# A two-layer hybrid decoder: the last projection turned to token order, single copies of cumulative sums, two float32 weight tiles for four, and another order in the mixers

## The chip, the cores and the metric

The kernel runs on one core of a Trainium2 chip. The metric is device time in microseconds (us) of one execution; lower is better. TensorE does the matrix products (PE in the profile, PEld for the load of its stationary operand), VectorE (DVE) and ScalarE (ACT) the elementwise work, GpSimd (POOL) a few fills, and SyncE (SP) issues all DMAs.

## The reference

A decoder trunk of two layers on 272 tokens (16 learned ones in front of 256), width 1024, float32. Each layer is a half-step SwiGLU, a mixer of three kinds of heads that run side by side, and another half-step SwiGLU, each followed by a LayerNorm of alpha times the stream plus the new part:

```python
for l in range(DEPTH):                                   # DEPTH = 2
    h = layer_norm(ALPHA * h + 0.5 * swiglu(h, gate1, up1, down1), ln1_g, ln1_b)
    proj = h @ w_in[l]
    z, xbc, dt_raw, fq, fk, fv, f_raw, cq, ckv, k_rope = split(proj)
    y_ssd = ssd_mixer(z, xbc, dt_raw, ...)               # state space, 8 heads, causal convolution before
    y_fox = fox_mixer(fq, fk, fv, f_raw, ...)            # attention with a forgetting bias, 4 heads
    y_mla = mla_mixer(cq, ckv, k_rope, ...)              # attention over latent keys, 4 heads
    mix = concatenate([y_ssd, y_fox, y_mla]) @ w_out[l]
    h = layer_norm(ALPHA * h + mix, ln2_g, ln2_b)
    h = layer_norm(ALPHA * h + 0.5 * swiglu(h, gate2, up2, down2), ln3_g, ln3_b)
return h[:, 16:]                                         # the 16 learned tokens are dropped
```

## The kernel before

Activations lie feature by feature: 128 features on the partitions, 272 tokens along the row, 8 such tiles for the width (22 for the inner width of a SwiGLU). A product takes 128 x 128 weights as the stationary operand and 272 tokens as the moving one; in layer 1 some run on 256 tokens, since the learned ones are no longer needed. To get near float32 from the faster float32r format, weights and activations are split into a high and a low part, and `pe3` (lines 363 to 365) makes three products for one: high by high, low by high, high by low. The split of weights is two instructions per 512 columns: a cast on ACT (`whi<-wraw`) and a subtraction on DVE (`wlo<-wraw,whi`). Four tiles of the mixers' input projection (`WHOLE`) are not split: `pe` (line 353) multiplies them as plain float32, and each such product stands in the trace as two records.

All instructions are put in order when the program is built, by a small scheduler (`Issue`). The program's parts are generators that hand it operations; it keeps a queue for each engine, takes the ready one of lowest priority number (`PR`), and gives an operation that may run on several engines to the one that it holds for least loaded. What comes out is a fixed order for each engine. On the chip an engine works its list in that order and waits where an operand isn't ready. The names in this document: `MORDER` is the order in which the tiles of the input projection are computed, `NUI` the number of those that start before the LayerNorm's statistics are known (they are corrected afterwards from two extra columns, hence 274 columns), `NUF` the same for pairs of gate and up tiles of a SwiGLU; `YORDER` is the order in which the eight parts of the mixers' output enter the output projection (0 to 3 state space, 4 and 5 the forgetting attention, 6 and 7 the latent attention), and `NPRE` the number of output tiles whose first four parts are multiplied ahead, as filler between the attention's steps.

In a mixer, `steps` turns one tile into softplus values (`sp`) by a chain of some 25 small operations; a product with a mask gives their running sums (`cu`). `copied` copies one row of these sums to all partitions by a product with a picked column (`cuh,identr` and `cul,identr`, lines 373 and 374). `Ct,Bt` are the scores of the state space, `m,z` its output products, `km,qm` and `fk,fq` the attention scores, `cs,s` transposes of probabilities, `sM,...` and `sT,...` the products with values, `inv,scr` the sums of squares of a root mean square, and `diag,ones` spreads one number per token over all partitions.

The last SwiGLU's down projection is made as all others: 8 output tiles by 22 inner tiles by 3 products of 256 columns. The LayerNorm after it (`Norm` with `last`) sums the tiles and their squares along the way (`zs`, `q`), multiplies both by a column of 1/1024, takes a square root on ACT and one Newton step, spreads the result, and scales the eight tiles on DVE, ACT and POOL; six DMAs write them.

Of the kernel before, what the change touches and what calls it, by code (L numbers as in the profile page):

```python
# [8 lines left out]
F32 = mybir.dt.float32  # L9
F32R = mybir.dt.float32r  # L10
# [6 lines left out]
P = 128  # L17
# [22 lines left out]
PR = dict(tail=2, shift=0, finish=0, means=1.5, whole=4, gated=3, front=0, soon=1, later=8, copies=5, head=4,  # L40
          meta=4, pair=7, state=1, group=7, steps=5, rope=1, linear=7, latent=8, conv=5.5, gate=0, query=4.5,
          scores=7.5, bytoken=0)

NSOON = 2
# [3 lines left out]
NUF, NUI = 6, 7  # L48
# [3 lines left out]
NPRE = 2  # L52
YORDER = (0, 1, 6, 7, 4, 5, 2, 3)
# [12 lines left out]
for _name, _w in (  # L66
# [50 lines left out]
class Issue:  # L117
# [5 lines left out]
    LAG = 0.13  # L123
# [42 lines left out]
    def resume(self, p):  # L166
# [6 lines left out]
        if isinstance(r, list):  # L173
            p[2] = len(r)
            for op in r:

                lag = 0.0 if op.eng == "t" and p[3] == "t" else self.LAG
# [111 lines left out]
def hybrid_trunk(ctx: ExitStack, tc: tile.TileContext, xt, wgu1, wd1, wgu2, wd2, win, wuq,  # L289
# [69 lines left out]
    def pe3(ps, a, b, start, stop):  # L359
# [7 lines left out]
        return Op("t", 3 * (ps.shape[-1] / 2400 + 0.0125), fn)  # L367

    def pe2(ps, a, bh, bl):


        def fn():
# [3 lines left out]
        return Op("t", 2 * (ps.shape[-1] / 2400 + 0.012), fn)  # L376
# [7 lines left out]
    for l in range(DEPTH):  # L384
        def plan_ffn(n, wgu, wd):
# [7 lines left out]
        plan_ffn(1, wgu1, wd1)  # L393
# [9 lines left out]
        plan_ffn(2, wgu2, wd2)  # L403
# [23 lines left out]
    def chunk(i, key, src, n, whole):  # L427
# [7 lines left out]
        yield D.dma_start(raw[:, :n], in_=src)  # L435
# [59 lines left out]
    identr = cpool.tile([P, 12], F32R, name="identr")  # L495
# [24 lines left out]
    def constants():  # L520
        yield [D.dma_start(pv, in_=pvec), D.dma_start(cs, in_=cst)]
        yield S.copy(identr, ident[:, :12])
# [36 lines left out]
    def spread(col, t0, sign, eng=("vgs",) * 3):  # L559

# [4 lines left out]
        for i, (a, b) in enumerate(token_tiles(t0)):  # L565
# [4 lines left out]
            ops.append(either(*[op for op in turn if op.eng in eng[i]]))  # L570
# [8 lines left out]
    class Norm:  # L579
# [4 lines left out]
        def __init__(self, l, which, coef, t0, u, x, last=False):  # L584
            self.l, self.which, self.coef, self.t0, self.u, self.x, self.last = l, which, coef / ALPHA, t0, u, x, last
# [21 lines left out]
        def front(self, t, ps):  # L607

            zt = z[:, t, self.tk]
            if self.last and t == 0:  # L610
                yield S.activation(self.st, ones[:, :8], AF.Sqrt)
# [4 lines left out]
        def tail(self, i):  # L616
# [4 lines left out]
            if self.last and i == KD - 1:  # L621
                self.mark("rest", 0)
                spawn(self.finish(zi, sq), PR["finish"])
            ops = [square(sq, zi)]
            if not self.last:
                g = pcol(self.l, self.which + "_g", i)
                uh, ul = self.u[0][:, i, self.tk], self.u[1][:, i, self.tk]
                ops.insert(0, scaled(uh, zi, g))
            yield ops
            if not self.last:  # L630
                yield V.scalar_tensor_tensor(ul, zi, g, uh.bitcast(F32), ALU.mult, ALU.subtract)
            self.mark("u", i)
            if self.last and i == KD - 1:
                self.mark("rest", 1)
                return
# [13 lines left out]
        def finish(self, *rest):  # L649
# [5 lines left out]
            spawn(self.means(*rest), PR["means"])  # L655

            nb = 2 * k if rest else 1
            yield take("bank", nb)
            pm = [bank() for _ in range(k)] if rest else [bank()] * k
            pq = [bank() for _ in range(k)] if rest else pm  # L660

            def sums(to, s, i, start, stop):
                a, b = tt[i]
                return to[i][:b - a, i:i + 1], s[:, a - self.t0:b - self.t0], inv[:, 0:1], start, stop

            tiles = range(k)
            po = [p[:, 4:] for p in pq]
            if rest:
                yield self.need(*[("sum", j) for j in range(KD - 1)], ("rest", 0))
                yield pe(*[sums(pm, self.zs, i, True, False) for i in tiles],  # L670
                         *[sums(po, self.q, i, True, False) for i in tiles],
                         *[sums(pm, rest[0], i, False, True) for i in tiles])
                yield self.need(("rest", 1))
                yield pe(*[sums(po, rest[1], i, False, True) for i in tiles])
                self.mark("msums")
                give("scr")
            else:
                yield pe(*[sums(pm, self.zs, i, True, True) for i in tiles],
                         *[sums(po, self.q, i, True, True) for i in tiles])
            msq, var = self.st[:, 0, :k], self.st[:, 1]  # L680
            if rest:
                parts = [(slice(0, P), slice(i, i + 1)) for i in tiles]
            yield [S.activation(msq[p, c], pm[c.start][p, c], AF.Square) for p, c in parts]
            yield [V.tensor_sub(var[p, c], po[c.start][p, c], msq[p, c]) for p, c in parts]
            give("bank", nb)
            var = var[:, :k]
            yield V.tensor_scalar(var, var, 0.0, EPS / ALPHA ** 2, op0=ALU.max, op1=ALU.add)
            r = yield from rsqrt(var, k, self.last)
            self.mark("root")
            if self.last:  # L690
                self.r = yield from spread(r, self.t0, 1.0, "vv")
                self.mark("stats")
                return
# [11 lines left out]
        def means(self, *rest):  # L705
# [3 lines left out]
            if not rest:  # L709
                yield pe((ps, ones, self.zs, True, True))  # L710
                yield scaled(self.nm, ps, -1.0 / 1024)
                give("bank")
                self.mark("nm")
                return
            yield self.need(*[("sum", j) for j in range(KD - 1)], ("rest", 0))
            yield pe((ps, ones, self.zs, True, False))
            yield self.need(("msums",))
            yield pe((ps, ones, rest[0], False, True))
            self.sums = ps
            yield S.mul(self.nm, ps, -1.0 / 1024)  # L720
            for ts in ((4, 6), (6, 8)):
                spawn(self.centred(*ts), PR["whole"] + 0.1 * ts[0])
            yield self.need(("root",))
            spawn(self.centred(0, 4), PR["whole"])

        def several(self, a, ts):

# [895 lines left out]
```

## Time and profile before

| what | value |
|---|---|
| runs | 1100.49, 1103.49 and 1104.07 us; median 1103.49 |
| profiled execution | 1102.75 us; its span from first to last instruction 1101.0 us |
| TensorE busy | 1081.2 us of the span (98%) |
| VectorE, ScalarE, GpSimd busy | 745.2, 620.4 and 7.3 us |
| granted TensorE clock, mean | 0.99 |
| DMA | 157 GB/s over the span, all on one queue of SP |

Busy time of TensorE counts a matmul from its start to its modelled end. Matmuls overlap, so a stretch can be busy throughout and still hold fewer matmuls than another of the same length; the number of matmuls in a stretch says more than the busy share. The granted clock is 1.0 at 2.4 GHz and 0.5 at 1.2 GHz.

### The profile page before, as it was taken

The page shows a single profiled execution, that of the slowest core. Times are in us where ns is not written, and L with a number is a line of the kernel's source. Part 1 is how long each engine was busy: PE and PEld are TensorE (multiplying, and loading weights), DVE is VectorE, ACT ScalarE, POOL GpSimd, SP SyncE. Part 2 cuts the span into 40 slices and gives each one's busy share as a digit, 9 for nine tenths or more (in the row PEclk, how much of TensorE's full clock was granted, in tenths as well). Part 3 has the DMA queues.
Part 4 walks back from the last instruction along what each step waited for, and adds up shares of the span by engine and source line. Part 5 has one row for each costly group of instructions (what it writes and reads, how often), then busy time and mean ns, then how long its engine had stood idle before and what let it go on. Part 6 is the DMA issues. An engine that isn't in the chain of part 4 may idle for free.

```text
span 1101.0 us, 21395 instructions
## 1 busy us (share of the span) xinstructions
PE 1081.2 (98%) x8340; PEld 1053.9 (96%) x8340; DVE 745.2 (68%) x1749; ACT 620.4 (56%) x1448; POOL 7.3 (1%) x18
## 2 busy tenths in 40 slices
PE   8999999999999999999999999999999999999996
PEld 8999999988979999999999999999899799999995
DVE  5655556688778985555679555565888589755563
ACT  6544444466876664444566444444768667645541
POOL 0000000000000000000000000000000000000000
PEclk9999999998999999999999999999999999999998
DMA  8655556515314275556526655564262153755641
GB/s 286 230 173 173 167 173 177 173 57 177 109 52 135 90 229 195 176 159 175 184 97 214 205 173 165 171 183 154 66 200 90 39 173 123 248 185 180 178 142 39
DMA packets 50997, 173.86 MB, mean 158 GB/s; under 512 B 5584, under 2 KB 8272, under 8 KB 50896
## 3 DMA queue, kind: packets, MB, share of 16 engines
q1 hardware_dynamic: 50896, 172.50, 49.8%
q8 instruction: 65, 1.06, 0.4%
q14 instruction: 36, 0.29, 0.1%
HBM read 171.43 MB, written 1.05 MB: 157 GB/s over the span
## 4 chain that ended last, share of the span: by engine, by line
PE 93%; ACT 4%; DVE 2%; issue 0%; DMA 0%; SPq 0%; DVEq 0%; ACTq 0%
PE bank L363 28%; PE bank L365 28%; PE bank L364 28%; PE bank L353 7%; ACT s L279 1%; PE bank L355 1%; DVE wlo L279 1%; DMA wraw<-in_wgu_dram 0%; ACT whi L279 0%; ACT km L279 0%; ACT scr L279 0%; DVE z L279 0%; ACT sT L279 0%; DVE scr L279 0%; PE bank L373 0%
## 5 line engine op out<-in xcount | busy, mean ns | idle before, releaser
L279 ACT CAST whi<-wraw 128x512 fp32r<-128x512 f32 (+2 forms) x648 | 376.0, 607 | 354.1 <-issue 278.4
L279 DVE TENSOR_TENSOR wlo<-wraw,whi 128x512 fp32r<-128x512 f32 (+2 forms) x648 | 421.7, 673 | 184.8 <-ACT whi L279 183.0
L363 PE MATMUL bank<-x0h,whi 128*128 128x272 f32 (+3 forms) x1220 | 353.2, 290 | 2.9 <-ACT whi L279 1.6
L365 PE MATMUL bank<-x0l,whi 128*128 128x272 f32 (+3 forms) x1220 | 350.5, 287 | 0.2
L364 PE MATMUL bank<-x0h,wlo 128*128 128x272 f32 (+3 forms) x1220 | 349.4, 286 | 0.5 <-DVE wlo L279 0.3
L363 PEld LDWEIGHTS bank<-x0h,whi 128*128 128x128 f32 x1220 | 231.1, 189 | 5.0 <-ACT x0h L279 2.5
L365 PEld LDWEIGHTS bank<-x0l,whi 128*128 128x128 f32 x1220 | 230.5, 189 | 1.3 <-DVE x0l L279 1.3
L364 PEld LDWEIGHTS bank<-x0h,wlo 128*128 128x128 f32 x1220 | 230.4, 189 | 1.3 <-DVE wlo L279 1.1
L363 PE MATMUL bank<-hh,whi 128*128 128x272 f32 (+1 forms) x704 | 202.3, 287 | 0.0
L365 PE MATMUL bank<-hl,whi 128*128 128x272 f32 (+1 forms) x704 | 201.3, 286 | 0.0
L364 PE MATMUL bank<-hh,wlo 128*128 128x272 f32 (+1 forms) x704 | 201.1, 286 | 0.0
L363 PE MATMUL bank<-x1h,whi 128*128 128x272 f32 (+3 forms) x592 | 174.0, 294 | 0.0
L365 PE MATMUL bank<-x1l,whi 128*128 128x272 f32 (+3 forms) x592 | 171.6, 290 | 0.0
L364 PE MATMUL bank<-x1h,wlo 128*128 128x272 f32 (+3 forms) x592 | 171.5, 290 | 0.0
L364 PEld LDWEIGHTS bank<-hh,wlo 128*128 128x128 f32 x704 | 132.6, 188 | 0.0
L363 PEld LDWEIGHTS bank<-hh,whi 128*128 128x128 f32 x704 | 132.5, 188 | 0.0
L365 PEld LDWEIGHTS bank<-hl,whi 128*128 128x128 f32 x704 | 132.5, 188 | 0.0
L363 PEld LDWEIGHTS bank<-x1h,whi 128*128 128x128 f32 x592 | 113.2, 191 | 0.5
L364 PEld LDWEIGHTS bank<-x1h,wlo 128*128 128x128 f32 x592 | 113.2, 191 | 0.3
L365 PEld LDWEIGHTS bank<-x1l,whi 128*128 128x128 f32 x592 | 113.3, 191 | 0.0
L279 DVE TENSOR_TENSOR scr<-scr,bank 128x272 f32<-128x272 f32 (+1 forms) x70 | 30.4, 434 | 68.7 <-PE bank L365 68.7
L279 DVE SCALAR_TENSOR_TENSOR z<-bank,hs 128x272 f32<-128x272 f32 (+1 forms) x48 | 20.9, 435 | 36.6 <-PE bank L365 36.4
(241 smaller groups left out, 945.9 us busy)
## 6 DMA issues: line engine op xcount, KB each, us to landing
wraw<-in_wgu_dram SPq DMA_DIRECT2D x174, 512.0 KB, 4.1
wraw<-in_wd_dram SPq DMA_DIRECT2D x64, 448.0 KB, 3.4
wraw<-in_win_dram SPq DMA_DIRECT2D x40, 512.0 KB, 3.4
wraw<-in_wd_dram SPq DMA_DIRECT2D x32, 512.0 KB, 3.5
wraw<-in_wout_dram SPq DMA_DIRECT2D x16, 512.0 KB, 3.7
wraw<-in_wuq_dram SPq DMA_DIRECT2D x2, 512.0 KB, 3.5
cs<-in_cst_dram SPq DMA_DIRECT2D x1, 856.5 KB, 6.9
hs<-in_xt_dram SPq DMA_DIRECT2D x3, 272.0 KB, 5.5
```

The lines of the kernel that those rows point to most:

```text
L279: op = Op(self.eng, self.cost(name, out, aps), lambda: getattr(self.to, name)(out, *args, **kw), table)
L353: nc.tensor.matmul(j[0], j[1], j[2], start=j[3], stop=j[4])
L355: nc.tensor.transpose(*j)
L363: nc.tensor.matmul(ps, a[0], b[0], start=start, stop=False)
L364: nc.tensor.matmul(ps, a[1], b[0], start=False, stop=False)
L365: nc.tensor.matmul(ps, a[0], b[1], start=False, stop=stop)
```

## The change

The down projection of the last SwiGLU is made by token (`by_token`): the stationary operand is a block of 128 tokens by 128 inner features, and the moving one 512 columns of weights, so that two blocks of tokens by two halves of the width fill four banks. The weights come in chunks of 4 output tiles by 2 inner ones, in rows of 256 floats. The stream is transposed into token order (`turned`), the LayerNorm is taken along the row with `bn_stats`, and each quarter of a block is transposed back, scaled and written by four DMAs. The last `NLAST` = 4 chunks are computed first for one block, then for the other. `copied` makes one product for two: the high part lies on rows 0 to 11 and the low part on rows 32 to 43 of one tile (`cub`), and the picked column (`both`) has a one in each. Two float32 tiles remain of four. `MORDER`, `YORDER`, the priorities, `NUF`, `NUI` and `NPRE` differ, and the scheduler holds a wait of 0.2 us instead of 0.13 behind an operation of TensorE.

```diff
-NSOON = 2
+NSOON = 3
-NUF, NUI = 6, 7
+NUF, NUI = 7, 8
+NLAST = 4
+LOW = 32
-NPRE = 2
-YORDER = (0, 1, 6, 7, 4, 5, 2, 3)
+NPRE = 3
+YORDER = (0, 7, 1, 6, 4, 3, 2, 5)
-MORDER = (M_Z + 3, M_Z + 1, M_B, M_FK, M_XS + 2, M_CQ, M_XS + 1, M_SMALL, M_XS + 3, M_CQ + 1, M_C, M_CKV, M_Z, M_XS,
-          M_FQ + 1, M_Z + 2, M_FV, M_FQ, M_FV + 1, "uq", "ukv", M_FK + 1)
-WHOLE = (M_SMALL, M_XS + 3, M_CQ + 1, M_C)
+MORDER = (M_XS + 1, M_Z + 1, M_CKV, M_Z + 3, M_CQ, M_XS + 2, M_XS, M_Z + 2, M_B, M_SMALL, M_FK, M_XS + 3, M_Z, M_CQ + 1, M_C, M_FK + 1, M_FQ + 1, M_FV, M_FV + 1, "uq", "ukv", M_FQ)
+WHOLE = (M_SMALL, M_C, )
...
-    LAG = 0.13
+    LAG, DRAIN = 0.13, 0.2
...
-            nc.tensor.matmul(ps, a, bh, start=True, stop=False)
-            nc.tensor.matmul(ps, a, bl, start=False, stop=True)
+    def pe1(ps, a, b):
+        return Op("t", ps.shape[-1] / 2400 + 0.0125, lambda: nc.tensor.matmul(ps, a, b, start=True, stop=True))
...
+            if last:
+                for h in range(2):
+                    for c in range(KF // 2):
+                        plan((l, n, "d", h, c), wd[l, 4 * h:4 * h + 4, :, 2 * c * P:2 * (c + 1) * P]
+                             .rearrange("d p c -> p d c"), 8 * P)
+                return
...
-            yield scaled(cuh[R], cu)
-            yield V.tensor_sub(cul[R], cu, cuh[R].bitcast(F32))
+            yield scaled(cub[R], cu)
+            yield V.tensor_sub(cub[LOW:LOW + 12], cu, cub[R].bitcast(F32))
```

`by_token` is new. `turned` transposes four tiles into a bank and copies them to `zt`; `front` adds a bank to it and takes the statistics; `quarter` normalises, transposes back and scales:

```python
def front(b, h, ps):
    zs = zt[:, b, h * 512:(h + 1) * 512]
    yield need((key, "turned", b, h))
    yield V.scalar_tensor_tensor(zs, ps, coef, zs, ALU.mult, ALU.add)
    give("bank")
    yield Op("v", 0.6, lambda: nc.vector.bn_stats(st[:, b, h], zs))
    mark(key, "stats", b, h)
...
def products(c, bs):
    w = [t.rearrange("p (d k x) -> p k d x", d=4, k=2) for t in weights[l, n, "d", h, c]]
    for i in range(2):
        k = 2 * c + i
        yield need(((l, "ffn", n), k), *[("w", (l, n, "d", h, c), j) for j in range(8)])
        for b in bs:
            a = [t[:, k, b * P:(b + 1) * P] for t in (hh, hl)]
            yield pe3(banks[b].rearrange("p (d x) -> p d x", d=4), a, [t[:, i] for t in w], k == 0, k == KF - 1)
```

How the instructions move, at three places. Line numbers differ by one between the two programs.

TensorE in the mixers of layer 0, before, from the running sums' products (`cs,sp`) on, with the last row in front of them:

```order
L365 MATMUL bank<-x1l,whi 128x272
L353 MATMUL bank<-cs,sp 12x272
L353 MATMUL bank<-cs,sp 12x144
L353 MATMUL bank<-cs,sp 12x16
...
L355 MATMUL bank<-cs,cu 128x12 x4
L355 MATMUL bank<-cs,cu 16x12 x2
L353 MATMUL bank<-Ct,Bt 128x272
L353 MATMUL bank<-Ct,Bt 128x144
L353 MATMUL bank<-Ct,Bt 16x16
L353 MATMUL bank<-inv,scr 128x1 x2
L353 MATMUL bank<-inv,scr 16x1
```

The left-out rows are six products of a projection tile. The same place in the change; the left-out rows are products of projection tiles (6, 9 and 9) and transposes `cs,xs`:

```order
L366 MATMUL bank<-x1l,whi 128x272
L354 MATMUL bank<-cs,sp 12x272
L354 MATMUL bank<-cs,sp 12x144
L354 MATMUL bank<-cs,sp 12x16
L356 MATMUL bank<-cs,xs 128x128 x4
...
L356 MATMUL bank<-cs,cu 128x12 x4
L356 MATMUL bank<-cs,cu 16x12 x2
...
L354 MATMUL bank<-Ct,Bt 128x272
L354 MATMUL bank<-Ct,Bt 128x144
L354 MATMUL bank<-Ct,Bt 16x16
```

The small products that stood together are now apart, with tiles of the projection between them, and the sums of squares (`inv,scr`) no longer stand here.

TensorE at the end of the mixers of layer 1, before, where the last head's probabilities (`cs,s`) are transposed and multiplied with the values; `x0h` with `whi` is the output projection:

```order
L355 MATMUL bank<-cs,s 128x128 x5
L353 MATMUL bank<-sM,df 128x256
L353 MATMUL bank<-sT,vf 128x256
L353 MATMUL bank<-sT,vf 128x128
L353 MATMUL bank<-sT,vf 128x256
L353 MATMUL bank<-sT,vf 128x128
L363 MATMUL bank<-x0h,whi 128x256
```

The same place in the change:

```order
L356 MATMUL bank<-cs,s 128x128 x2
L364 MATMUL bank<-x0h,whi 128x256
L365 MATMUL bank<-x0h,wlo 128x256
L366 MATMUL bank<-x0l,whi 128x256
...
L354 MATMUL bank<-sM,df 128x256
L354 MATMUL bank<-sT,vf 128x256
L354 MATMUL bank<-sT,vf 128x128
L354 MATMUL bank<-sT,vf 128x256
L354 MATMUL bank<-sT,vf 128x128
L364 MATMUL bank<-x0h,whi 128x256
```

Six products of the output projection stand between the transposes and the products that need their copy, and what follows the last `sT,vf` begins with parts 3 and 2 of the output, where before it began with part 5, which those products make.

VectorE at the end of the program in the change, for the second block of tokens:

```order
L280 SCALAR_TENSOR_TENSOR z<-bank,z 128x512
L814 BN_STATS bnst<-z 128x6
L823 BN_AGGR bn_mv<-bnst 128x2
L280 TENSOR_SCALAR bn_ve<-bn_mv 128x1
...
L280 TENSOR_TENSOR rs_a<-rs_13399 128x1
L280 SCALAR_TENSOR_TENSOR rs_a<-rs_a,bn_ve 128x1
L280 SCALAR_TENSOR_TENSOR rs_y<-rs_a,rs_13399 128x1
L280 SCALAR_TENSOR_TENSOR bn_nm<-bn_mv,rs_y 128x1
L280 TENSOR_SCALAR z<-z,rs_y,bn_nm 128x256 x2
L280 TENSOR_SCALAR hs<-bank,pv 128x128 x4
```

The row left out is a reciprocal, which waits for a square root on ACT. Before, the end of VectorE's list was the chain of `lnst` and `rs`, two `diag`, and ten operations on `z` of 256 to 1024 columns.

## Rows read from the trace of the kernel before

**Rows 1.** The page, part 1: busy us of each engine.

```profile
span 1101.0 us, 21395 instructions
...
PE 1081.2 (98%) x8340; PEld 1053.9 (96%) x8340; DVE 745.2 (68%) x1749; ACT 620.4 (56%) x1448; POOL 7.3 (1%) x18
```

**Rows 2.** Stages: length, busy us (x instructions) of PE, PEld, DVE, ACT, POOL; clock; DMA.

```profile
209.40:354.00 144.60, 142.32 (x980) 129.84 (x979) 112.53 (x363) 98.44 (x270) 2.31 (x6) 0.98 0.33 107
...
757.80:897.20 139.40, 135.32 (x947) 123.94 (x946) 107.39 (x330) 98.37 (x267) 2.31 (x6) 0.99 0.34 109
...
1024.80:1086.80 62.00, 62.00 (x531) 62.00 (x530) 30.89 (x59) 25.01 (x50) 0.00 (x0) 1.00 0.43 125
1086.80:1101.00 14.20, 4.02 (x24) 2.85 (x22) 8.93 (x20) 4.13 (x10) 2.48 (x2) 0.71 0.22 74
```

**Rows 3.** Stretches of products alone: 272 columns (first) and 256 columns.

```profile
440.00:540.00 100.00, 100.00 (x797) 100.00 (x796) 57.50 (x108) 47.32 (x99) 0.00 (x0) 1.00 0.57 171
...
1030.00:1080.00 50.00, 50.00 (x429) 50.00 (x428) 27.12 (x52) 22.39 (x45) 0.00 (x0) 1.00 0.47 136
```

**Rows 4.** Timeline of TensorE: start, us, engine, line, operation; float32 tiles of layer 0.

```profile
232.87 8.87 PE L353 MATMUL bank<-hs,wraw 128*128 128x272 f32 x38
241.67 0.72 PE L353 MATMUL bank<-scr,cs 64*128 64x272 f32 x2
```

**Rows 5.** Groups of TensorE by shape: the copies of sums.

```profile
L373 PE MATMUL bank<-cuh,identr 128*128 128x272 f32 x24 | 7.1, 308 | 0.0
```

**Rows 6.** Stretches at half clock, in both layers' mixers.

```profile
260.00:263.40 3.40, 3.40 (x13) 2.84 (x13) 1.34 (x5) 0.62 (x1) 0.00 (x0) 0.50 0.51 161
263.40:266.80 3.40, 3.40 (x17) 3.13 (x16) 2.41 (x11) 0.00 (x0) 0.00 (x0) 0.50 0.19 71
809.50:812.90 3.40, 3.40 (x17) 3.40 (x17) 2.95 (x12) 0.05 (x1) 0.00 (x0) 0.50 0.44 131
```

**Rows 7.** Waits of TensorE in layer 0's mixers: us in total, times, longest.

```profile
PE bank L353 <- DVE sp L279: 0.7, 1, 0.7
PE bank L353 <- ACT sM L279: 0.5, 1, 0.5
PE bank L363 <- ACT x0h L279: 0.5, 1, 0.5
```

**Rows 8.** The same in layer 1's mixers.

```profile
PE bank L353 <- ACT sM L279: 1.1, 2, 0.7
PE bank L353 <- ACT diag L279: 0.9, 2, 0.6
PE bank L353 <- DVE sp L279: 0.8, 1, 0.8
```

**Rows 9.** Timeline of TensorE, layer 1: transposes, whose operand is read with a stride.

```profile
873.24 0.75 PE L355 MATMUL bank<-cs,s 128*128 128x128 f32 x5
```

**Rows 10.** Groups of TensorE by shape: weights as the moving operand.

```profile
L363 PE MATMUL bank<-whi,x0h 128*128 128x256 f32 x4 | 1.3, 323 | 0.0
```

**Rows 11.** Groups of VectorE and ScalarE by shape, 1080 us to the end: busy us, mean ns.

```profile
L279 DVE TENSOR_SCALAR diag<-cs,rs_y 128x128 f32<-128x128 f32 x2 | 2.6, 1320 | 0.0
...
L279 DVE TENSOR_TENSOR z<-z,bank 128x512 f32<-128x512 f32 x2 | 1.3, 680 | 0.0
...
L279 DVE TENSOR_SCALAR z<-z,pv 128x256 f32<-128x256 f32 x3 | 1.1, 409 | 0.0
...
L279 DVE TENSOR_SCALAR lnst<-lnst 128x2 f32<-128x2 f32 x1 | 0.2, 171 | 0.0
...
L279 ACT ACTIVATE z<-z,pv 128x256 f32<-128x256 f32 x5 | 2.8, 595 | 4.8 <-DVE z L279 4.8
...
L279 ACT ACTIVATE rs<-lnst 128x2 f32<-128x2 f32 x1 | 0.2, 203 | 0.7 <-DVE lnst L279 0.7
```

**Rows 12.** Timeline of the end, VectorE's last operation, and landing of the output DMAs.

```profile
1097.32 0.41 DVE L279 TENSOR_SCALAR z<-z,pv 128x256 f32<-128x256 f32 x1
...
out_dram<-z SPq DMA_DIRECT2D x2, 256.0 KB, 2.3
```

More of the change, by code (lines that the diff above doesn't have):

```diff
@@ L38 @@
 PAIR = True
-PR = dict(tail=2, shift=0, finish=0, means=1.5, whole=4, gated=3, front=0, soon=1, later=8, copies=5, head=4,
-          meta=4, pair=7, state=1, group=7, steps=5, rope=1, linear=7, latent=8, conv=5.5, gate=0, query=4.5,
-          scores=7.5, bytoken=0)
-NSOON = 2
+PR = dict(tail=3, finish=6, means=1.5, whole=4, gated=1, front=5, soon=1.5, later=8, copies=7, head=0, meta=8, pair=2, state=6, group=8, steps=5, rope=1.5, linear=8, latent=0.5, conv=7, gate=1, query=4, scores=0.5, bytoken=0)
+NSOON = 3
 DCUT = ((0, 8), (8, 15), (15, 22))
-NUF, NUI = 6, 7
+NUF, NUI = 7, 8
 NSCR, NS = 9, 3
-NPRE = 2
-YORDER = (0, 1, 6, 7, 4, 5, 2, 3)
+NLAST = 4
+LOW = 32
+NPRE = 3
+YORDER = (0, 7, 1, 6, 4, 3, 2, 5)
 FOX_SCALE = 64 ** -0.5
@@ L494, in hybrid_trunk @@
     ident = cc("ident")
-    identr = cpool.tile([P, 12], F32R, name="identr")
+    both = cpool.tile([P, 12], F32R, name="both")
     turns = cpool.tile([P, 2], F32, name="turns")
@@ L569, in spread @@
                     *([S.mul(to, by, v)] if sign == 1.0 else [])]
-            ops.append(either(*[op for op in turn if op.eng in eng[i]]))
+            ops.append(either(*turn))
         yield ops
@@ L620, in tail @@
             sq = scr(self.n)
[L621 to L631, printed above, removed]
+            g = pcol(self.l, self.which + "_g", i)
+            uh, ul = self.u[0][:, i, self.tk], self.u[1][:, i, self.tk]
+            yield [scaled(uh, zi, g), square(sq, zi)]
+            yield V.scalar_tensor_tensor(ul, zi, g, uh.bitcast(F32), ALU.mult, ALU.subtract)
             self.mark("u", i)
-            if self.last and i == KD - 1:
-                self.mark("rest", 1)
-                return
             if i == 0:
@@ L654, in finish @@
             parts = [(slice(0, P), slice(0, 2))] + [(slice(0, 16), slice(2, 3))] * (k - 2)
[L655 to L679, printed above, removed]
@@ L680, in finish @@
-            msq, var = self.st[:, 0, :k], self.st[:, 1]
[L681 to L685, printed above, removed]
+            spawn(self.means(), PR["means"])
+            yield take("bank")
+            ps = bank()
+            yield pe(*[(ps[:b - a, 4 * j + i:4 * j + i + 1], s[:, a - self.t0:b - self.t0], inv[:, 0:1], True, True)
+                       for j, s in enumerate((self.zs, self.q)) for i, (a, b) in enumerate(tt)])
@@ L686, in finish @@
+            msq, var = self.st[:, 0, :k], self.st[:, 1]
+            yield [S.activation(msq[p, c], ps[p, c], AF.Square) for p, c in parts]
+            yield [V.tensor_sub(var[p, c], ps[p, 4 + c.start:4 + c.stop], msq[p, c]) for p, c in parts]
+            give("bank")
             var = var[:, :k]
             yield V.tensor_scalar(var, var, 0.0, EPS / ALPHA ** 2, op0=ALU.max, op1=ALU.add)
[L688 to L693, printed above, removed]
+            r = yield from rsqrt(var, k)
@@ L703, in normalise, with means @@
                 spawn(self.whole(t), PR["whole"] + 0.1 * t)
-        def means(self, *rest):
+        def means(self):
             yield take("bank")
             ps = bank()[:, :self.n]
[L709 to L724, printed above, removed]
@@ L741, in left @@
[L741 to L756 removed]
+            yield pe((ps, ones, self.zs, True, True))
@@ L758, in whole @@
+            yield scaled(self.nm, ps, -1.0 / 1024)
+            give("bank")
+            self.mark("nm")
         def whole(self, t):
@@ L851, in ffn @@
                 yield norm.need(*[("x", t) for t in range(KD)])
+            if nxt is None:
+                yield from by_token(l, n, norm, hh, hl)
+                return None
             nxt = nxt()
-            if not nxt.last:
-                spawn(nxt.columns())
+            spawn(nxt.columns())
             for t in range(KD):
```

133 lines of the change are left out of this document (86 added, 47 removed).

## The prediction

> **What bounds the kernel now.** I read the page first: the span is 1101.0 us and TensorE counts as busy for 98% of it [rows 1]. The profiled execution took 1102.75 us, 1.75 us more than its span and 0.74 us less than the median of the runs shown. So time can be won in two ways only: fewer or shorter instructions on TensorE, or a shorter stretch at the end, where TensorE has done its work.
>
> A busy TensorE is not one at its peak, so I then took the stages and compared counts. Where it makes nothing but split products, 100 us hold 797 of 272 columns, 125.6 ns each, and 50 us hold 429 of 256 columns, 116.8 ns each [rows 3]. (A window also counts the one that it cuts, hence 796 and 428.) A float32 product is two records, and 38 records of 272 columns take 8.80 us from their start to that of the next row, so 232 ns a record and 463 ns a product [rows 4]. A transpose of 128 columns costs about 0.11 to 0.12 us: five of them are busy for 0.75 us, of which some 0.27 is the drain of the last [rows 9].
>
> With these prices I add up the mixers. In the order of layer 0 they hold 639 split products and copies (80.3 us at 125.6 ns), 70 wide float32 products (58 x 463 and 12 x 432 ns, the latter 2 x 216 in proportion to columns: 32 us), 19 of 144 columns (4.7 us), 49 short ones of two records (10.8 us, at the 0.11 us of a transpose for each) and 63 transposes (6.9 us): about 134.5 us. The stage lasts 144.6 us [rows 2], so some 10 us are lost. Layer 1 gives about 128 of 139.4 us [rows 2], 11 us lost. Some 21 us in all, against none in the SwiGLUs.
>
> Where do they go? First, 10.2 us pass at half clock [rows 6]: 13 and 17 matmuls in 3.4 us where the rate above gives 27, so about 5.1 us lost. Before both falls TensorE did a thin run of work: it waited for `sp`, and then made masks, 64-row scores and one-column sums with few split products between. Second, waits for single operations: `sp` 0.7 and 0.8 us, copies of `sM` 0.5 and 1.1, the split of the last output part (`x0h`) 0.5, `diag` 0.9 [rows 7, 8]. Each also costs the drain of the matmul before it, some 0.15 us, which the profile calls busy. The rest, 8 to 10 us, is smaller gaps that no row names.
>
> At the end, the last products are issued by 1086.8 us and the span runs 14.2 us longer [rows 2].
>
> **The change, part by part.**
>
> *Single copies of sums.* Each layer copies 12 rows; each copy loses one of two products: 24 x 125.6 ns = 3.0 us. They stand in TensorE's stream [rows 5], nothing hides them, and nothing is added but a small sum that builds the picked column. Bounds: 2 to 3, since a copy on which TensorE then waits gives less.
>
> *Two float32 tiles less per layer.* Eight products of 463 ns become eight times three of 125.6 ns: 86 ns each, 0.7 us for a tile of 272 columns, 0.6 for the one of 256. Over two tiles and two layers: 2.7 us. In exchange ACT and DVE split four more tiles, two halves of 512 columns a tile at some 680 ns on DVE [rows 11], 2.7 us a layer. The mixers leave DVE 32 us free in each layer [rows 2], so I price that at nothing; where it delays a chain it could cost up to those 2.7 us in each layer.
>
> *More early tiles.* One more pair in three SwiGLUs and one more tile in two mixers carry two more columns: 192 products by about 0.55 ns a column (the slope between the two rates) by 2: 0.2 us more.
>
> *The last projection.* Before: 528 products of 256 columns in 62.0 us [rows 2]. After: 264 of 512 columns. No row shows 512. The 256-column product costs 116.8 ns, of which 106.7 are columns at 2.4 GHz, so 10.1 ns come on top. If these come once per product, 512 columns cost 223.4 ns and the whole 59.0 us; if they grow with the columns, 61.7. I take 59.0, since a fixed part is what the rows with few columns suggest too. That weights are the moving operand is known to cost no more: such a product stands beside the others with the same mean [rows 10], and an operand read with a stride runs at full pace [rows 9]. The stage gains 16 transposes of the stream and 8 of the first block, 24 x 0.11 = 2.7 us. Together 61.7: no change; bounds are 2.7 more and, were the fixed part below 3 ns, 2 less.
>
> The page "TensorE: Matmul & The Clock Gate" of the Trainium skill, section "Back-to-back issue gap", gives a warm gap of N/2.4 + 2.5 ns. For 256 columns that is 109.2 ns, and the trace shows 116.8 here. By the rule 512 columns would cost 215.8 ns, the stage 57.0 us and the whole forecast 2 us less.
>
> A chunk must now be complete before its first product. Behind that wait stands the whole projection; the cover is six split tiles ahead and a DMA share of 0.43 in this stage [rows 2]. Rows of 1 KB instead of 4 KB have room there.
>
> *The first block's end.* Its eight transposes stand before the last six products. Its chain must fit into the 18 products before them, 4.0 us; by the sum below the last quarter is ready at 4.5 us, while the earlier ones take their 0.7 us. I price it at nothing; at worst 0.6 us.
>
> *The tail.* After the last product: 0.2 us to the first DVE operation, 0.68 for the add from the bank [rows 11], the same 0.68 for the statistics (no row shows `bn_stats`; bounds 0.4 and 1.2 from the other rows of this group), then two small ones, a square root on ACT (0.20), five small ones, at 0.17 each and 0.03 between [rows 11]: 3.2 us. Then two quarters on DVE (0.41 each) and two on ACT (0.60 each): 4.5. Transposes run in their shade. ACT's four scalings out of the bank stand last: about 0.5 each between 0.6 and the small rows, 6.5 us. Then one DMA: it lands 2.3 us after issue [rows 12], and 1.05 us more to the end: before, VectorE's last operation ended at 1097.73 us and the span 3.3 us later [rows 12]. In all 9.9 us for 14.2: 4.3 us won. What goes away are the two `diag`, 1.32 us each beside GpSimd [rows 11], and the passes over eight tiles. Bounds: 8.8 to 11.5.
>
> *The order in the mixers.* The thin run is broken up: masks, scores and `cu` now have tiles of the projection between them, and the sums of squares went elsewhere. I count the falls of the clock as gone: 5.1 us. The products between the start of `steps` and `cs,sp` grow from some 12.3 to 15.2 us in layer 0, which covers the 0.7 us wait and its drain; layer 1 alike: 1.7 us together. At the end of both layers six products stand between `cs,s` and `sM`, and the part that arrives last is multiplied last: of the `sM` and `x0h` waits I count 2.2 us as gone. That is 9 us. What is late next: `diag` and the one `sM` of layer 1 that still has no cover; those I leave. New waits of the new order can't be read from a trace of the old one. Bounds: nothing won, and 18 of the 21 us.
>
> **Sum.** 3.0 + 2.7 - 0.2 + 0 + 4.3 + 9.0 = 18.8 us less than 1102.75: **1084 us**.
>
> **Rivals.**
>
> *The order gains nothing.* Other waits take the place of the old ones; the free 32 us of DVE are an average, and in the attention steps it is not free. Then 10 us of the sum remain: 1093. For it: two more tiles to split and one more early tile fall on DVE early in each mixer. Against: fillers stand where the longest waits were.
>
> *Most of the lost time returns.* The gaps without a name shrink as well, since an order with more filler helps all: 18 instead of 9 us: 1075. Against: DVE and ACT are still taken in turn, and a chain of dependent steps has a length.
>
> *The clock falls elsewhere.* In layer 0 the change puts latent and forgetting attention side by side without a split product between for some 12 us by the prices above (`cs,s`, `sM`, `fk,fq`). Both falls of before came after a thin run [rows 6]; against it, a run of the same kind, some 5 us, stands in the old order and kept its clock. One fall of the lengths seen costs 1.7 to 3.4 us, in both layers up to 7: 1086 to 1091. The same page of the Trainium skill, section "PE-mode transpose", says that transposes don't count as busy for the clock, which speaks for this rival; the trace shows no fall in the old order's transposes.
>
> *Slower.* 512 columns of strided weights don't run at one column a cycle. The point at which the kernel becomes slower is 223 + 19000 / 264 = 295 ns a product; at two cycles a column, as float32 has them [rows 4], it would be 427 ns, 54 us more: 1138. Against it stand rows 9 and 10, so I give it little.
>
> **Chances.** Forecast 0.50 (1079 to 1088), order gains nothing 0.17, most returns 0.13, clock falls elsewhere 0.15, slower 0.05. Going from the forecast to 1074 below and 1095 above leaves out the slower rival, part of those 18 us and the case in which several bounds fall together, under 0.2. A change of 0.3% (3.3 us) is about what a measurement of this kernel can tell from none. All cases but the last lie over it: faster 0.92, same 0.04, slower 0.04.
>
> **What would show it.** In the profile after: 264 products of 512 columns at about 223 ns; half the copies; no stretch of half clock in the mixers; the waits for `sp` gone and those for `sM` shorter; mixers of about 137 and 132 us; a tail of some 10 us from the last product. The prediction fails if the mixers hold as much lost time as before, if half clock shows up elsewhere, or if 512 columns cost much over 230 ns.

## Result and the profile after

The changed kernel takes 1085.38 us, the median of four runs (1084.51 to 1086.30), against 1103.61 for the kernel before. The ratio, taken over all runs, is 0.9841, with a 95% interval of 0.9820 to 0.9862, or 17.5 us less; it differs a little from that of the two medians, and what a run gives is worked out from its ratio below. The forecast was 1084. The profiled execution took 1086.02 us, 16.7 less than that of before.

The page's part 1 of the kernel after, against [rows 1]: TensorE loses 246 instructions and 13.9 us of busy time, and is still the bound.

```profile
span 1084.2 us, 20897 instructions
...
PE 1067.3 (98%) x8094; PEld 1034.8 (95%) x8094; DVE 749.3 (69%) x1770; ACT 625.2 (58%) x1455; POOL 4.3 (0%) x14
```

The stages of the kernel after, with the columns of [rows 2]: mixers of layer 0, of layer 1, last projection, tail. The last row, of TensorE alone, is the stretch of half clock in layer 1.

```profile
209.70:346.30 136.60, 134.97 (x983) 125.43 (x983) 114.05 (x370) 100.98 (x274) 2.04 (x5) 1.00 0.32 111
749.40:883.90 134.50, 130.50 (x951) 121.43 (x950) 109.97 (x338) 100.95 (x269) 2.04 (x5) 0.99 0.34 111
1011.60:1074.70 63.10, 63.10 (x290) 51.95 (x288) 29.97 (x55) 25.95 (x48) 0.00 (x0) 1.00 0.38 117
1074.70:1084.20 9.50, 1.23 (x9) 0.86 (x8) 4.65 (x15) 2.92 (x8) 0.00 (x0) 0.79 0.38 110
...
844.66:848.07 3.41, 3.41 (x16) 0.50 0.38 132
```

Against [rows 2] the mixers give 8.0 and 4.9 us, the tail 4.7, and the last projection takes 1.1 back: 16.5 of the 16.7 us. The falls of the clock of [rows 6] are gone, but layer 1 has a new one of the same length, with 16 matmuls in 3.41 us where some 27 should be. TensorE's idle time, the length of a stage less its busy time, fell from 2.3 to 1.6 us in layer 0 and stayed in layer 1 (4.1 and 4.0): of the 12.9 us, 0.7 are idle time, and the rest was busy time before.

The waits of TensorE in the mixers of the kernel after, layer 0 and layer 1 (us in total, times, longest):

```profile
PE bank L354 <- DVE scr L280: 1.0, 1, 1.0
PE bank L354 <- ACT sM L280: 0.2, 1, 0.2
...
PE bank L354 <- DVE scr L280: 1.6, 1, 1.6
PE bank L354 <- DVE sM L280: 1.0, 1, 1.0
PE bank L364 <- DVE cd L280: 0.8, 1, 0.8
PE bank L354 <- ACT sM L280: 0.6, 1, 0.6
```

The waits for `sp` and `x0h` of [rows 7, 8] are gone, and that for `sM` in layer 0 is down from 0.5 to 0.2 us. In layer 1, `sM` has risen from 1.1 to 1.6. What is late now is `scr`, the sum of two squared tiles ahead of the one-column sums. Waits and fall stand together: TensorE waited at 840 for `scr`, at 843 for `sM`, and the clock fell at 844.66.

The timeline of the tail, VectorE, ScalarE and TensorE of the kernel after:

```profile
1074.47 0.40 PE L366 MATMUL bank<-wlo,hh 128*128 128x512 f32 x1
...
1074.90 0.69 DVE L280 SCALAR_TENSOR_TENSOR z<-bank,z 128x512 f32<-128x512 f32 x1 [0.67 <-PE bank L366]
1075.63 0.69 DVE L814 BATCH_NORM_STATS2 bnst<-z 128x6 f32<-128x512 f32 x1
1076.35 0.21 DVE L823 BATCH_NORM_AGGREGATE bn_mv<-bnst 128x2 f32<-128x12 f32 x1
...
1078.00 1.09 ACT L280 ACTIVATE z<-z,bn_nm,rs_y 128x256 f32<-128x256 f32 x2 [1.01 <-DVE bn_nm L280]
...
1078.56 1.06 PE L356 MATMUL bank<-cs,z 128*128 128x128 f32 x8 [3.70 <-DVE z L280]
...
1079.45 1.50 ACT L280 ACTIVATE hs<-bank,pv 128x128 f32<-128x128 f32 x4 [0.36 <-DVE hs L280]
```

The statistics take 0.69 us, the same as the add ahead of them; ScalarE's last scaling ends at 1080.95 and the span 3.3 us later, as before.

### The profile page after: what moved, and what is told of

The parts are those of the page before. It is cut to its first block, busy times and chain, and to the rows that moved or that the text cites. A ratio compares the mean times of both kernels' runs of the same rounds, so it can differ in the third digit from the quotient of the medians.

```text
span 1084.2 us, 20897 instructions
## 1 busy us (share of the span) xinstructions
PE 1067.3 (98%) x8094; PEld 1034.8 (95%) x8094; DVE 749.3 (69%) x1770; ACT 625.2 (58%) x1455; POOL 4.3 (0%) x14
## 4 chain that ended last, share of the span: by engine, by line
PE 92%; DVE 4%; ACT 3%; DMA 1%; issue 0%; SPq 0%; ACTq 0%
PE bank L364 29%; PE bank L366 28%; PE bank L365 28%; PE bank L354 5%; PE bank L356 1%; DVE wlo L280 1%; ACT s L280 1%; DMA wraw<-in_win_dram 1%; DVE scr L280 1%; DMA hs<-in_xt_dram 1%; ACT m L280 1%; ACT whi L280 0%; SPq L277 0%; DVE xs L280 0%; DVE m L280 0%
## 5 line engine op out<-in xcount | busy, mean ns | idle before, releaser
L364 PE MATMUL bank<-x1h,whi 128*128 128x272 f32 (+3 forms) x624 | 182.2, 292 | 0.0
L366 PE MATMUL bank<-x1l,whi 128*128 128x272 f32 (+3 forms) x624 | 179.4, 288 | 0.0
L365 PE MATMUL bank<-x1h,wlo 128*128 128x272 f32 (+3 forms) x624 | 179.1, 287 | 0.0
L366 PE MATMUL bank<-hl,whi 128*128 128x272 f32 x528 | 152.6, 289 | 0.0
L365 PE MATMUL bank<-hh,wlo 128*128 128x272 f32 x528 | 152.3, 288 | 0.0
L364 PE MATMUL bank<-hh,whi 128*128 128x272 f32 x528 | 151.5, 287 | 0.0
L364 PEld LDWEIGHTS bank<-hh,whi 128*128 128x128 f32 x528 | 99.9, 189 | 0.0
L366 PEld LDWEIGHTS bank<-hl,whi 128*128 128x128 f32 x528 | 99.4, 188 | 0.0
L365 PEld LDWEIGHTS bank<-hh,wlo 128*128 128x128 f32 x528 | 99.1, 188 | 0.0
L280 ACT CAST hh<-scr 128x272 fp32r<-128x272 f32 (+1 forms) x88 | 36.3, 413 | 20.0 <-DVE scr L280 19.9
```

What stands on the lines that cost most here:

```text
L280: op = Op(self.eng, self.cost(name, out, aps), lambda: getattr(self.to, name)(out, *args, **kw), table)
L364: nc.tensor.matmul(ps, a[0], b[0], start=start, stop=False)
L365: nc.tensor.matmul(ps, a[1], b[0], start=False, stop=False)
L366: nc.tensor.matmul(ps, a[0], b[1], start=False, stop=stop)
```

## Experiments

**One part at a time.** Each of the first four is the kernel before with one part of the change. Each ratio is against the kernel before, run beside it; what a part gives is worked out from the ratio.

Last projection: `by_token`, the plan of its weights and their DMA are taken over, the rest stays.

```diff
-        plan_ffn(2, wgu2, wd2)
+        plan_ffn(2, wgu2, wd2, l == DEPTH - 1)
+            if nxt is None:
+                yield from by_token(l, n, norm, hh, hl)
```

> The kernel before with nothing but the new last projection by token and its tail; tables, copies and float32 tiles as before. If the terms add up as read from the two traces: products and transposes of the stage 1.1 us longer (63.1 for 62.0), tail 4.7 us shorter (9.5 for 14.2), so 3.6 us less than before, about 1100.0 us (ratio 0.9967), mixers within 1 us of 144.6 and 139.4. Rival: half tiles of the last projection arrive later without the new priorities, TensorE waits in the stage, and 2 us or less are won (1101.6 or more).

Measured: 1098.31 us, ratio 0.9964 (0.9949 to 0.9979), so 4.0 us less. The stage takes 63.1 us and the tail 9.6. The profiled execution is the shortest of the twelve, at 1094.84 us; it has 3.4 us of half clock in the mixers where [rows 6] have 10.2.

Tables:

```diff
-PR = dict(tail=2, shift=0, finish=0, means=1.5, ...
+PR = dict(tail=3, finish=6, means=1.5, ...
-NSOON = 2
+NSOON = 3
...
-NUF, NUI = 6, 7
+NUF, NUI = 7, 8
...
-NPRE = 2
+NPRE = 3
-YORDER = (0, 1, 6, 7, 4, 5, 2, 3)
+YORDER = (0, 7, 1, 6, 4, 3, 2, 5)
```

(`MORDER` and `DRAIN` change as well, as shown above.)

> The kernel before with only the new tables: priorities, order of tiles and output parts, more early tiles, and the longer lag behind TensorE; four float32 tiles, double copies and the old last projection (with its old priorities) stay. Theory of the prediction: fillers cover the waits, 9 less 0.2 us won; read from the two traces with 3.0 and 2.7 for copies and tiles it would be 7.2: 1094.8 to 1096.5 us. Rival one: copies and tiles were only exchanged against waits, then the tables alone give all 12.9 us of the mixers: about 1090.7. Rival two: the tables fit only the shorter chains, and the order alone gives under 4 us: over 1099.6.

Measured: 1095.69, ratio 0.9937 (0.9917 to 0.9956), 6.9 us less. Its profile has no half clock in layer 0, and 3.4 us of it in layer 1, from 857.6 on.

Copies:

```diff
-            yield pe2(ps, identr[:, r:r + 1].to_broadcast([P, P]), cuh, cul)
+            yield pe1(ps, both[:, r:r + 1].to_broadcast([P, P]), cub)
```

> The kernel before with single copies of the sums alone: 24 products of 272 columns fewer. If they stand in TensorE's stream unhidden, 3.0 us less: 1100.6 (ratio 0.9973), and both mixers are 1.5 us shorter. Rival: the copies stand in chains on which TensorE waits anyway, under 1 us is won (over 1102.6) and the idle time behind them grows instead.

Measured: 1098.12, ratio 0.9966 (0.9953 to 0.9979), 3.7 us less. Its profile has no half clock in the mixers, and they are 3.7 and 2.8 us shorter, not 1.5 each. So the saved products and the clock both have a share: over all executions the mean granted clock is 0.9916, against 0.9894 in those of the kernel before beside it, and executions of the two at the same granted clock differ by 1.8 to 2.9 us (0.988 to 0.993).

Float32 tiles:

```diff
-WHOLE = (M_SMALL, M_XS + 3, M_CQ + 1, M_C)
+WHOLE = (M_SMALL, M_C, )
```

> The kernel before with two float32 tiles per layer, not four, and nothing else. If TensorE's count decides, 2.7 us less: 1100.9 (ratio 0.9976). Rival one: the four tiles that DVE and ACT now split cost the chains 1 to 2 us in a layer, and the time stays within 1 us of before. Rival two: what is won is more than 2.7 us since fewer slow products also change when the chains start.

Measured: 1100.07, ratio 0.9985 (0.9972 to 0.9998), 1.7 us less. Its trace shows what takes part of the gain: a wait in layer 0 that [rows 7] don't have, and a stretch of half clock in layer 1 as long as both layers' in [rows 6]; layer 0 has none.

```profile
PE bank L363 <- ACT cd L279: 2.7, 1, 2.7
...
805.14:815.38 10.24, 10.24 (x46) 0.50 0.34 106
```

The four sum to 16.3 us; together they gave 17.5, and 16.5 in a second set of runs (ratio 0.985, below). That looks as if the terms simply added up. The next run shows that they don't.

**All but the tables.** The changed kernel with the tables of before (the second diff, reversed).

> The changed kernel with the old tables (priorities, order of tiles and output parts, early tiles, lags); new last projection, single copies and two float32 tiles stay. If the terms add up as measured one by one (4.0 for the last projection, 3.7 for copies, 1.7 for tiles): 9.4 us less than before, about 1093.2 (ratio 0.9915). Rival: each set of instructions needs an order of its own; the old tables with the new instructions then lose several us to new waits, and the time is 1096 or more, while the new tables are worth over 10 us here for 6.9 alone.

Measured: 1099.90, ratio 0.9982 (0.9966 to 0.9999). Three parts that gave 9.4 us one by one give 2.0 together, and the new tables are worth some 14.5 us or more on top of them. The waits of its layer 0, and its stretches at half clock there, in an execution of 1103.64 us (lines are numbered otherwise in this kernel). The last two rows are the way from the last product of a layer's first SwiGLU to the first down product of its second, layer 0 and layer 1; under them the same two in the changed kernel:

```profile
PE bank L358 <- ACT diag L284: 2.8, 1, 2.8
PE bank L358 <- ACT sM L284: 2.4, 2, 1.7
PE bank L358 <- DVE sp L284: 1.1, 1, 1.1
...
256.41:266.65 10.24, 10.24 (x48) 0.50 0.37 107
300.78:307.61 6.83, 6.03 (x28) 0.50 0.02 8
324.67:334.91 10.24, 9.31 (x34) 0.50 0.01 2
...
208.59:498.57 289.98, 281.26 (x2058) 0.95 0.41 133
766.25:1028.99 262.74, 259.04 (x2019) 1.00 0.46 148
```

```profile
209.53:481.80 272.27, 270.64 (x2057) 1.00 0.43 142
749.31:1011.62 262.31, 258.31 (x2019) 0.99 0.45 148
```

At half clock TensorE does half the work at most, so 27.3 us cost up to 13.7 in this execution. All of what the old tables lose in it stands in layer 0 (17.7 us); layer 1 is only 0.4 us longer than with the new ones. Its twelve times lie in two groups, 1095.7 to 1098.4 at a mean granted clock of 0.988 to 0.993, and 1101.4 to 1104.2 at 0.983 to 0.987; which falls the shorter ones are spared no profile shows.

**No float32 tile.** The changed kernel with `WHOLE = ()`.

> The changed kernel without the two float32 tiles that are left in each layer (all tiles split into two halves). By TensorE's count another 2.7 us are won: about 1083. By what two tiles gave alone (1.7 us): 1084. Rival: these two tiles spare DVE and ACT their splits where the chains run; then the chains become later and the time is the same or up to 2 us more than the changed kernel.

Measured: 1097.95, ratio 0.9957 (0.9941 to 0.9973): 12 us slower than the changed kernel, although TensorE has less to do: the rival's direction, at six times its size. The plan, made anew for two more split tiles, puts TensorE behind the root of a norm and behind `sM`; layer 0 waits at 290 and at 308 us, and the clock falls behind each (at 294.2 and 311.2). The run doesn't tell apart what the splits delay and what the other plan does:

```profile
PE bank L353 <- DVE rms L279: 3.3, 1, 3.3
PE bank L353 <- ACT sM L279: 1.9, 1, 1.9
```

**The price of 512 columns.**

```diff
+                        src = wd[l, 4 * h:4 * h + 4, :, 2 * c * P:2 * (c + 1) * P]
+                        plan((l, n, "d", h, c), src.rearrange("d p c -> p d c") if h else
+                             src.rearrange("d p (k x) -> p k d x", k=2), 8 * P)
...
-                        yield pe3(banks[b].rearrange("p (d x) -> p d x", d=4), a, [t[:, i] for t in w],
-                                  k == 0, k == KF - 1)
+                        to = banks[b].rearrange("p (d x) -> p d x", d=4)
+                        for o in ((0, 2), (2, 4)) if h and 0 < k < KF - 1 else ((0, 4),):
+                            yield pe3(to[:, o[0]:o[1]], a, [t[:, i, o[0]:o[1]] for t in w], k == 0, k == KF - 1)
```

> The changed kernel with two other forms of the last projection: in its first half the weights lie in the order in which they are read (each chunk loaded by two DMAs), so the 512 columns have no stride; in its second half all but the first and last products are two of 256 columns. Measured in the changed kernel: 229 ns for 512 columns with a stride. If the stride costs the 5.6 ns over my 223.4, the first half falls to 223 ns, 0.7 us less. If the part above the columns grows with their number, the first half stays at 229. Second half: two of 256 at 116.8 ns are 233.6 ns, 0.6 us more than 229. Both changes together: within 1 us of the changed kernel.

Measured: 1086.35 us. Stretches of products alone: the changed kernel, and then this one, first half (512 without a stride) and second half (256 with one). A window also counts those cut at its ends.

```profile
1015.00:1070.00 55.00, 55.00 (x242) 1.00 0.40 125
...
1015.00:1040.00 25.00, 25.00 (x111) 1.00 0.69 197
1045.00:1070.00 25.00, 25.00 (x211) 1.00 0.14 43
```

From start to start, the 512-column products take 229.6 ns on average in both kernels, with the stride and without, so at 512 columns the stride costs nothing. The 256-column ones take 118.1. The line through both widths is 6.6 ns plus 0.436 ns a column, which gives 125.2 ns at 272 columns, where [rows 3] have 125.6; columns at 2.4 GHz would take 0.417. With the 116.8 ns of [rows 3] at 256 columns it would be 4.0 ns plus 0.441.

**The clock in layer 1.** The changed kernel once more, as the base of the next runs:

> The changed kernel once more, unchanged, as the base for the three that share its chip, and for a second profile. If the place where the clock falls is set by the order of the work, the fall of 3.4 us in layer 1's mixers stands again within a few us of 844.7, and layer 0 has none. Rival: the falls come and go between executions of one kernel; then this profile has it elsewhere or not at all, and differs by about 1.7 us from 1086.02.

Measured: 1085.85 (1084.05 to 1086.55), and the fall of layer 1 stands at 849.70, in a trace that runs 2.3 us early: 7 us later in the program. That is in the same thin run, but not at the same instruction.

```profile
849.70:853.11 3.41, 3.41 (x14) 0.50 0.12 42
```

The 2.3 us come from the start, where the clock of this execution stays up once it has risen, while in the first it falls again for 3.4 us at 11.8 us; matmul by matmul, this one is 2.2 us ahead from 16 us on. Both need 134.5 us for the mixers of layer 1.

Twelve dummies in one wait:

```diff
+            one = pe1(pt[:, 16:16 + T], both[:, 0:1].to_broadcast([P, P]), cub)
+            yield Op("t", sums.us, lambda: [op.fn() for op in [one] * more + [sums]])
...
+            r = yield from rms(sq, 1, t0, 12 if (l, g) == (1, 1) else 0)
```

> The changed kernel with 12 more copies of the sums in layer 1 (into a bank region that is written over afterwards; nothing reads them), put right ahead of the one-column sums for which TensorE waited 1.62 us before the clock fell; order of all else unchanged. Theory: the thin run ahead of the fall brings it about; 1.5 us of dummies fill the wait, cost nothing, and the clock stays: 1.7 us less than the changed kernel, about 1084. Rival one: the fall has another cause, the dummies only take up the wait: same time within 0.3 us and the fall stays. Rival two: the wait is not real slack, the dummies come on top: 1.5 us more.

Measured: 1085.46 (1082.64 to 1085.68), within the spread of the changed kernel. The dummies cost nothing that the time shows, and the theory fails: the fall stays (10 matmuls in 3.41 us), 9 us after the filled wait, and the mixers of layer 1 take 134.9 us for 134.5:

```profile
850.44:853.85 3.41, 3.34 (x10) 0.50 0.35 108
```

Dummies in three waits, with 6 and 10 ahead of `sM` in latent attention besides the 12:

```diff
+            more = 0 if fox or not l else (6, 10)[c]
...
+            yield Op("t", mix.us, lambda: [op.fn() for op in [one] * more + [mix]])
```

> The changed kernel with dummies in three waits of layer 1's thin run: 12 copies of the sums ahead of the one-column sums, 6 ahead of the first and 10 ahead of the second mixing product of latent attention, for which TensorE waited 1.8, 0.7 and 1.4 us; nothing reads what they write, the order is unchanged. Theory: the fall comes from the whole thin run of some 14 us, which one filled wait did not end; with three filled the clock stays at full speed in layer 1 and 1.7 us are won, about 1084. Rival: other thin instructions (64-row scores, transposes) bring the fall about; it stays, same time as the changed kernel or up to 0.5 us more.

Measured: 1083.16 (1082.80 to 1084.51), ratio 0.9832 (0.9820 to 0.9845). The mixers of layer 1, from and to the same matmuls as above, have no half clock now and take 1.1 us less; under them two of the filled places in the timeline of TensorE:

```profile
748.70:882.10 133.40, 132.32 (x979) 1.00 0.34 112
...
840.03 1.76 PE L372 MATMUL bank<-cub,both 128*128 128x272 f32 x12 [0.26 <-ACT sT L280]
841.62 0.50 PE L354 MATMUL bank<-inv,scr 128*128 128x1 f32 x4
841.99 0.99 PE L372 MATMUL bank<-cub,both 128*128 128x272 f32 x6
842.82 0.59 PE L354 MATMUL bank<-sM,dm 128*128 128x256 f32 x2
```

28 useless instructions more, and a kernel that is rather faster: 1.0 to 2.0 us by the two ratios of the changed kernel (0.9841 and 0.985). The intervals overlap; two of the nine runs of the changed kernel (1084.05 and 1084.51) lie within the range of these four. The profiled execution is the longest of the four, and no shorter than the second of the changed kernel, as it has 3.4 us of half clock at the start. The transposes (`cs,s`) of the stretch ran at full clock, so they don't bring the fall about by themselves.

A shorter chain ahead of the same wait:

```diff
+            sums = pe(*[(pt[:b - a, i:i + 1], sq[:, a - t:b - t], inv[:, col:col + 1], j == 0, j == len(sqs) - 1)
+                        for i, (a, b) in enumerate(tt) for j, sq in enumerate(sqs)])
...
-                yield added(sqs[0], sqs[0], sqs[1])
+                was = added(sqs[0], sqs[0], sqs[1])
+                for op in (was, *was.others):
+                    op.fn = lambda: None
+                yield was
```

> The changed kernel without VectorE's addition of two squared tiles ahead of the one-column sums: TensorE sums both tiles into the same column instead (twice as many one-column products); plan and order of everything else unchanged. The addition stands last in the chain for which TensorE waited 1.0 us in layer 0 and 1.8 us in layer 1. Theory: the chain ends where ACT's squares end, so 0.4 to 0.8 us less for each of the two waits, 1 us in all: about 1085 (ratio 0.984 or less). Rival: VectorE's queue or the root behind the sums sets the end, and nothing is won, or the extra one-column products cost 0.1 us at each of six places: within 0.6 us of the changed kernel.

In this kernel the addition keeps its place in the plan and does nothing.

Measured: 1089.08 (1084.55 to 1091.36), ratio 0.9873 (0.9852 to 0.9894). The wait of 1.6 us is down to 0.4, as hoped, and the kernel is some 3 us slower. In its profile the clock falls twice in layer 1, whose mixers take 136.7 us for 134.5:

```profile
845.05:848.46 3.41, 3.41 (x12) 0.50 0.49 157
855.29:858.70 3.41, 3.41 (x15) 0.50 0.09 34
750.40:887.10 136.70, 133.39 (x964) 0.98 0.33 110
...
PE bank L354 <- ACT scr L280: 0.4, 1, 0.4
```

That is not the falls alone. Twice as many one-column products cost 0.4 to 0.5 us at each of four places where TensorE doesn't wait, not the 0.1 us expected: 12 of them take 1.24 us where 6 took 0.74. Of the 3.5 us by which this profile is longer than the first of the changed kernel, some 1.2 lie in the thin run with its two falls, and some 0.6 at the start, where this execution has 3.4 us more of half clock. The granted clock goes with the time: two of the six executions, of 1084.55 and 1084.59 us, have a mean of 0.996, and the four of 1088.68 to 1091.36 us have 0.990 to 0.992.

The same with dummies in the three waits (5, 8 and 11):

> The kernel without the additions, in whose profile the clock fell twice in layer 1's thin run, with dummy copies of the sums in the same three waits of layer 1 as before: 5, 8 and 11 for waits of 0.6, 1.0 and 1.4 us; nothing reads them, order unchanged. If the thin run brings the falls about, they go, and the kernel keeps what the missing additions gave: about 1083, 1 us less than with additions and dummies at best, and 6 us less than without dummies. Rival: that the falls were missing in the kernel with the three fillings was chance (executions of one kernel differ); then the falls stay and the time is 1088 to 1090.

Measured: 1085.66 (1083.98 to 1087.83), ratio 0.9845 (0.9827 to 0.9862): 3 us less than without the dummies, though the intervals overlap. Both falls of layer 1 are gone, and from and to the same matmuls its mixers take 2.9 us less (133.8 for 136.7). The time of 1083 isn't reached, since the one-column products cost what they cost before, and this execution, the longest of the five, has a fall in layer 0, which holds no dummies:

```profile
309.81:313.23 3.42, 3.42 (x11) 0.50 0.39 132
751.90:885.70 133.80, 132.97 (x987) 1.00 0.35 112
```

## Why the prediction was right, and where not

*Single copies.* 3.0 us were forecast and 3.7 measured alone (2.3 to 5.2). That fits products that stand in TensorE's stream, but doesn't show it alone: the granted clock rose as well, and at the same granted clock 1.8 to 2.9 us are left for the products.

*Two float32 tiles less.* 2.7 forecast, 1.7 measured alone (0.2 to 3.1). Pricing the exchange at nothing was too good: a wait of 2.7 us for `cd` came in, and with two tiles more the exchange turned into a loss of 12 us. Whether the extra splits delay the chains or the plan, made anew in both runs, puts TensorE behind them too early, is not shown: before, the last `m,z` and `m,xd` ran right ahead of the products of `cd`; in this run they were done nearly 6 us before TensorE came to them.

*The last projection.* 61.7 us forecast, 63.1 measured. The term of the products was mis-sized: all of the 10.1 ns above the columns were taken as fixed per product; by the line through both widths 4.0 to 6.6 are, and the rest grows with the columns. 264 x 229.6 ns are 60.6 us, not 59.0. The Trainium skill, "TensorE: Matmul & The Clock Gate", section "Back-to-back issue gap", gives N/2.4 + 2.5 ns for a single product at full clock, so 215.8 here; the measured 229.6 ns are 13.8 above it, and 118.1 ns at 256 columns are 8.9 above it.

*First block's end and tail.* The eight transposes of the first block waited for nothing. The tail took 9.5 us for 9.9. The statistics took 0.69 us where 0.68 was taken over from the add beside them; most of the difference is ACT's four scalings out of the bank, 1.5 us where 2.0 were said.

*The order.* With copies and tiles 14.5 us were forecast for the mixers, 12.9 came: 136.6 us where about 137 was said, and 134.5 for about 132. Both old falls went, as forecast. In layer 1 the rival came true by which the clock falls elsewhere (11 matmuls short, 1.4 us by the rate of [rows 3]), though the rival had named layer 0, which kept its clock. So the clock gave 3.7 us of the 5.1 counted. The waits gave less still: 3.9 us were counted for `sp`, `sM` and `x0h` with their drains, and TensorE's idle time fell by 0.7, as `scr`, `cd` and a longer `sM` took the place of those that went. With copies and tiles at their forecast prices the order gave some 7 us; the 3 us that are neither clock nor idle time come from busy time that no row names, which the prediction had left to its second rival.

*What failed* is that the terms are independent prices. The sum of 18.8 us was close to the 17.5 measured, but 9 us is not what the order is worth: it gives 6.9 alone and some 14.5 or more on top of the rest, and without it the other parts shrink from 9.4 to 2.0. The first rival, new waits in place of the old ones, describes the old tables under the new instructions, and the waits of the changed kernel too, whose time fell all the same. That the total came out so near is in part luck.

*The clock.* That thin runs of TensorE bring the falls about is supported: all five profiles with this stretch thin (the changed kernel twice, the one with one filled wait, the other products, the one without additions) have one or two falls there, between 844.7 and 858.7 us; both with three filled waits have none, and their mixers of layer 1 are 1.1 and 2.9 us shorter than their like. A thin run doesn't always bring one: a granted clock of 0.996, as in two executions without the additions, leaves some 9 us at half clock, and the tail of the profiled one alone has 7.1. Why an execution has a fall at one place of such a run and not at another stays open: layer 0 had one in one profile of seven with nearly the same order there.

## What to carry to other kernels

Don't price a new order and new instructions apart where chains on several engines alternate with one bound engine: measure the parts both alone and left out. Look at the granted clock around the waits before shortening a chain: a wait of 1.6 us cut to 0.4 won nothing here. Dummies in waits cost nothing that the time showed, and in two kernels of two the clock stayed up where three waits were filled; one filled wait didn't do it. For long, dense stretches take a price per column from two widths, not one.

## What the hardware showed unexpectedly

Executions of one unchanged kernel differ in where the clock falls. Two profiles of the changed kernel have it 7 us apart in the program, and one is 2.2 us ahead from 16 us on, since its clock kept up at the start. Falls of 3.4, 6.8 and 10.2 us were seen. The mean granted clock of an execution goes with its time: the 29 executions of the kernel before that ran beside the first four parts reach from 1099.23 us at 0.993 to 1106.64 us at 0.984. So compare the granted clocks of two kernels before giving a difference of a few us to their instructions. And a moving operand of 512 columns read in pieces of 128 costs nothing: 229.6 ns either way.
